# A two-layer hybrid decoder step: conditioning vectors computed one by one, compression units ahead of the first norm, window states copied DRAM to DRAM

## The chip, the cores and the metric

One core of a Trainium2 chip runs the kernel. The metric is the device time of one execution in microseconds; the time before is 1059.74 us, the median of three runs (1058.38 to 1064.3). A profile of one execution gives each engine's instructions with start and duration: PE (TensorE; PEld are its weight loads), DVE (VectorE), ACT (ScalarE), POOL (GpSimd) and SP (the queue that issues most DMAs).

## The reference, cut to what matters

Two layers over 264 token columns: a prompt of 256 and 8 samples of one token. Everything is fp32.

```
mod = silu(c) @ ada_w + ada_b            # (9 rows, 6*1024): sh1, sc1, g1, sh2, sc2, g2
h   = rmsnorm(x) * norm1_g * (1 + sc1) + sh1
proj = h @ w_in                          # q, 6 K/V blocks, gates, z, xBC, dt
kcmp, vcmp = compress(past + new K/V)    # per sample: 32-row blocks, stride 16, two-layer MLP
o_att = gated sum of three branches      # compressed, 16 selected blocks, sliding window of 512
y     = SSD scan over xBC, dt; gated norm with silu(z)
x  += g1 * (concat(o_att, y) @ w_out)
h2  = rmsnorm(x) * norm2_g * (1 + sc2) + sh2
x  += g2 * ((silu(conv3(h2 @ Wg)) * (h2 @ Wu)) @ w_down)
```

Outputs are also the new K/V rows, the scan states, the convolution states, and the sliding-window states of the samples. For the last, the kernel writes the old 512-row window as it is (`wst`, 2 layers x 8 samples of 128x1024, 512 KB each), and the new row is joined to it outside.

## The kernel before, in words

Activations lie as [128 features, 8 blocks, 264 tokens]. A weight tile is 128x1024 (512 KB); it is loaded into one of four `st` buffers, split into a high and a low part (`whi` by ACT, `wlo` by DVE, three buffers each), and used in 24 matmuls of 264 columns (three products for each of eight blocks).

`ada(l, r)` (line 303) computes the conditioning in three rounds r of two vectors each: round 0 gives sh1 and sc1, round 1 g1 and sh2, round 2 sc2 and g2. A round has eight steps, one for each k-block. A step loads four 256 KB tiles and makes four matmuls of 512 columns, each into another quarter of the PSUM partitions (32 columns of the array each, tile `psfl`). Each tile has its own load, buffer and wait. At the end of a round the result is copied (`adam`), transposed by four matmuls and put into `mod`. It is a generator: whoever calls next() on it places one step in the program.

`compress(l, both, bufs)` (line 376) summarizes the compressed-branch pages of the samples in eight units, keys and values in turn for each of four pairs of samples: a unit is 48 matmuls of 252 columns (`pso<-whi,cwh` and two more) and a small second step. With `both` the pages (`cpg`) come with K and V in one load of 128 KB each, 16 loads for a pair, and four buffers. Each of the two weights `cw` is 1 MB.

The order of layer 0: one unit and round 0 of the conditioning, the squares and norm 1; then the input projection (16 tiles `win`; line 462 on), with one unit and one step of round 1 ahead of each tile until they are used up; then the attention stage, where generators for samples (S), prompt (P), scan (M), blocks (B), gating (Z) and conditioning round 2 (A) are interleaved by a written order, `SEQ`; then the output projection, norm 2, and the FFN: up (22 pairs of `wup` tiles; ahead of every second pair one compression unit and one step of round 0 of layer 1), and down (22 `wdn` tiles, five steps of round 1 of layer 1). Layer 1: norm 1, three steps of round 1 (`GAP`), input projection, attention stage with round 2, output projection, norm 2, FFN.

In the attention stage the samples read three sets of eight pages through a ring of eight 512 KB buffers `page`: two sets of selected blocks, 32 loads of 128 KB each set, and the window state, one load for each sample, which is also stored to the output from that buffer (line 606):

```
            if i == 2:
                load(t, I["wst"][l, s])
                store(O["wst"][l, s], t)
```

Loads go through SP, stores through POOL; each engine takes its instructions in one fixed order, made ahead of time by the framework from the program's order and its own estimate of what is ready. Matmuls of other work can therefore stand between the four of one step. In the scan for the samples, four times a layer, DVE writes a masked copy `bd` (8x512, one buffer) that one matmul broadcasts.

Almost all instructions carry line 117, the wrapper that issues them, so the profile is read by tile names.

## Time and profile before

| | |
|---|---|
| time, median of 3 (lowest, highest) | 1059.74 us (1058.38, 1064.3) |
| the profiled execution | 1060.55 us, span 1058.8 us |
| PE busy | 979.6 us (93%) |
| DVE, ACT, POOL busy | 655.8, 486.3, 170.0 us |
| mean granted TensorE clock | 0.949 of full speed |
| DMA | 220.33 MB, mean 208 GB/s |

"Busy" is the time in which an engine has at least one instruction under way. An fp32 matmul leaves two records, the other kind of matmul (high and low parts) one. A row of the chain of waits names what the next instruction in the chain that ended last was held by; "DMA ada" there is the time from issue to landing.

### The profile page before, as it was taken

To read this page: it belongs to the slowest core of one execution; us is meant where nothing else is said; L and a number is where in the kernel's file an instruction comes from. 1 tells how busy PE (TensorE), PEld (TensorE's weight loads), DVE (VectorE), ACT (ScalarE), POOL (GpSimd) and SP (SyncE) were. 2 spreads that over 40 slices of the span, in tenths; PEclk is the share of its full clock that TensorE was granted. 3 is DMA by queue.
4 is the path that set the end of the run, shared out by engine and by line. 5 is a ranking of instruction groups with operands and counts; after the bars stand their busy time and mean duration, and the time that the engine had idled before them with its cause. 6 is when DMAs were issued, how large, how long until landed. Compare 5 with 4: busy or idle time off the path is not lost.

```text
span 1058.8 us, 20737 instructions
## 1 busy us (share of the span) xinstructions
PE 979.6 (93%) x7480; PEld 795.0 (75%) x7480; DVE 655.8 (62%) x1427; ACT 486.3 (46%) x1036; POOL 170.0 (16%) x337
## 2 busy tenths in 40 slices
PE   3799999997997999999999989999799789999996
PEld 3238898652466899899998949965246689999995
DVE  2347554557657865766764558365865777777553
ACT  3225544332254554655553426453235456666441
POOL 0201001114213000101111103031421311111110
PEclk9899999897899899999999999999789889999998
DMA  8779668436847777765577568753694635555651
GB/s 279 262 240 304 227 211 280 162 128 203 333 158 222 225 219 232 255 195 193 185 233 236 165 223 262 250 180 126 207 339 152 208 100 180 181 180 182 195 171 41
DMA packets 115081, 220.33 MB, mean 208 GB/s; under 512 B 13218, under 2 KB 56098, under 8 KB 114850
## 3 DMA queue, kind: packets, MB, share of 16 engines
q1 hardware_dynamic: 110882, 205.29, 60.5%
q0 software_dynamic: 3520, 13.17, 3.1%
q8 instruction: 59, 0.97, 0.4%
q10 hardware_dynamic: 576, 0.54, 0.2%
q14 instruction: 44, 0.36, 0.1%
HBM read 204.70 MB, written 14.25 MB: 207 GB/s over the span
## 4 chain that ended last, share of the span: by engine, by line
PE 82%; DMA 6%; DVE 6%; ACT 2%; issue 2%; SPq 2%; POOL 0%; DVEq 0%; ACTq 0%; POOLq 0%
PE psmm L117 42%; PE psat L117 23%; PE pso L117 10%; PE psfl L117 8%; DMA ada<-in_ada_dram 3%; SPq L117 1%; DMA st<-in_cw_dram 1%; DVE wlo L117 1%; DMA st<-in_wup_dram 1%; DVE bd L117 1%; DMA cpg<-in_cmpc_dram 1%; DVE rs L117 1%; ACT whi L117 1%; DVE psm L117 0%; DVE st L117 0%
## 5 line engine op out<-in xcount | busy, mean ns | idle before, releaser
L117 DVE TENSOR_TENSOR wlo<-st,whi 128x1024 fp32r<-128x1024 f32 (+1 forms) x204 | 232.7, 1141 | 148.8 <-ACT whi L117 132.9
L117 ACT ACTIVATE whi<-st 128x1024 fp32r<-128x1024 f32 (+1 forms) x204 | 201.8, 991 | 231.0 <-PE psmm L117 163.3
L117 PE MATMUL psmm<-hhi,whi 128*128 128x264 f32 x800 | 233.3, 292 | 4.2 <-ACT hhi L117 2.6
L117 PE MATMUL psmm<-hhi,wlo 128*128 128x264 f32 x800 | 228.4, 286 | 0.8 <-DVE wlo L117 0.8
L117 PE MATMUL psmm<-hlo,whi 128*128 128x264 f32 x800 | 228.6, 286 | 0.0
L117 PEld LDWEIGHTS psmm<-hhi,whi 128*128 128x128 f32 x800 | 151.5, 190 | 22.3 <-issue 7.4
L117 PEld LDWEIGHTS psmm<-hhi,wlo 128*128 128x128 f32 x800 | 151.2, 189 | 3.0 <-DVE wlo L117 1.6
L117 PEld LDWEIGHTS psmm<-hlo,whi 128*128 128x128 f32 x800 | 151.9, 190 | 0.9 <-issue 0.7
L117 PE MATMUL psmm<-act,whi 128*128 128x264 f32 x704 | 128.7, 284 | 0.0
L117 PEld LDWEIGHTS psmm<-act,whi 128*128 128x128 f32 x704 | 108.8, 188 | 4.2 <-issue 3.4
L117 PE MATMUL psfl<-ada,cs 128*32 128x512 f32 x384 | 99.3, 648 | 11.0 <-DMA ada<-in_ada_dram 10.9
L117 PE MATMUL psat<-hhi,whi 128*128 128x264 f32 x352 | 100.8, 286 | 1.4 <-ACT whi L117 1.4
L117 PE MATMUL psat<-hhi,wlo 128*128 128x264 f32 x352 | 100.6, 286 | 1.0 <-DVE wlo L117 1.0
L117 PE MATMUL psat<-hlo,whi 128*128 128x264 f32 x352 | 100.5, 286 | 0.0
L117 PE MATMUL psmm<-act,wlo 128*128 128x264 f32 x352 | 99.9, 284 | 0.0
L117 PE MATMUL pso<-whi,cwh 128*128 128x252 f32 x256 | 76.3, 298 | 21.0 <-ACT whi L117 16.2
L117 PE MATMUL pso<-wlo,cwh 128*128 128x252 f32 x256 | 75.5, 295 | 0.1
L117 PE MATMUL pso<-whi,cwl 128*128 128x252 f32 x256 | 75.3, 294 | 0.0
L117 PEld LDWEIGHTS pso<-whi,cwh 128*128 128x128 f32 x256 | 51.3, 200 | 31.6 <-ACT whi L117 16.2
L117 PEld LDWEIGHTS psat<-hhi,whi 128*128 128x128 f32 x352 | 67.1, 191 | 1.6 <-ACT whi L117 1.6
L117 PEld LDWEIGHTS psat<-hhi,wlo 128*128 128x128 f32 x352 | 66.8, 190 | 1.2 <-DVE wlo L117 1.2
L117 PEld LDWEIGHTS psat<-hlo,whi 128*128 128x128 f32 x352 | 67.2, 191 | 0.0
(303 smaller groups left out, 1553.2 us busy)
## 6 DMA issues: line engine op xcount, KB each, us to landing
ada<-in_ada_dram SPq DMA_DIRECT2D x192, 256.0 KB, 4.4
st<-in_wup_dram SPq DMA_DIRECT2D x88, 512.0 KB, 3.6
st<-in_wdn_dram SPq DMA_DIRECT2D x44, 512.0 KB, 3.5
st<-in_win_dram SPq DMA_DIRECT2D x40, 512.0 KB, 4.6
page<-in_slcc_dram SPq DMA_DIRECT2D x128, 128.0 KB, 2.6
st<-in_cw_dram SPq DMA_DIRECT2D x16, 512.0 KB, 5.4
cpg<-in_cmpc_dram SPq DMA_DIRECT2D x64, 128.0 KB, 3.3
st<-in_wout_dram SPq DMA_DIRECT2D x32, 256.0 KB, 3.0
```

The source lines that it names most:

```text
L117: ins = f(*a, **k)
```

## The change

The conditioning is computed by single vectors: `ada(l, js)` takes a list of vectors j of six. A step is now two k-blocks: two tiles of [4, 256] (512 KB each), and eight matmuls of 256 columns, which `together` keeps in order, the last-loaded tile first and the other seven at high priority. The buffers become 3, 2 and 4 of 512 KB where they were 6, 4 and 6 of 256 KB. A vector has four steps, two vectors eight. Vectors 0 and 1 stay ahead of norm 1 of layer 0 and in the FFN-up of layer 0 (for layer 1). Vectors 2 and 3 stay where round 1 was, with four steps in the FFN-down and no `GAP`: the other four come in the input projection of layer 1. Vector 4 is in the attention stage in layer 0 and in the input projection in layer 1; vector 5 is in the FFN-up of its own layer.

Four compression units (keys and values of two pairs of samples) stand ahead of the first norm where one did, with three, three, two and no conditioning steps behind them, and the squares behind the second. The first pair's pages are loaded keys first, values later, 64 KB each. In layer 1 the page ring's pool is opened before the input projection, and one page set is fetched per tile there. The window states are no longer stored from the ring; sixteen DRAM-to-DRAM copies, one for each of the third to eighteenth pairs of the last FFN-up, write them. The scan's four `bd` become two tiles of 8x1024, both written ahead of the loop.

```diff
-ADA_BUFS = {"cmp": 6, "att": 4, "ffn": 6}
+ADA_BUFS = {"cmp": 3, "att": 2, "ffn": 4}
+    def together(calls):
+        for n, (out, w, a, start, stop) in enumerate(calls):
+            if n == 0:
+                PE.matmul(out, w, a, start=start, stop=stop)
+                continue
+            with tc.high_priority():
+                tc.keep_in_program_order(PE.matmul(out, w, a, start=start, stop=stop))
-    def ada(l, r):
+    def ada(l, js):
...
-        acc = fl()
-        for k in range(KC):
-            for g in range(4):
-                t = sb([512], "ada", ADA_BUFS[name[:3]], F32, pools[-2] if name == "attn1" else pools[-1])
-                load(t, I["ada"][l, r * KC + k, :, g, :])
-                PE.matmul(acc[32 * g:32 * g + 32, :], cs[:, k, :], t, start=k == 0, stop=k == KC - 1)
-            yield
+        for j in js:
+            acc = fl()[:, :256]
+            for kk in range(0, KC, 2):
+                two = []
+                for k in (kk, kk + 1):
+                    t = sb([4, 256], "ada", ADA_BUFS[name[:3]], F32, pools[-2] if name == "attn1" else pools[-1])
+                    load(t, I["ada"][l, j, k])
+                    two.append((k, t))
+                together([(acc[32 * g:32 * g + 32, :], cs[:, k, :], t[:, g, :], k == 1, k == KC - 2)
+                          for k, t in reversed(two) for g in range(4)])
+                yield
...
             elif kv == 0:
-                pair = [pages(s, 0) for s in (2 * sp, 2 * sp + 1)]
+                pair = [pages(s, 0, 2 if sp else 1) for s in (2 * sp, 2 * sp + 1)]
+            elif sp == 0:
+                for s in range(2):
+                    load_pages(pair[s][:, :, 1:], I["cmpc"][l], s, 1, 1)
...
+        pb = begin(f"attn{l}") if early is None else None
...
+            if pb is not None and len(ring) < PAGES:
+                fetch()
...
                 load(t, I["wst"][l, s])
-                store(O["wst"][l, s], t)
...
+            bds = [ph([1024], "mam", 2) for _ in range(2)]
+            for g in range(2):
+                V.tensor_tensor(bds[g][:8].rearrange("p (b s n) -> p b s n", b=2, s=NS), ...)
...
-                    bd = small([NS, 64], 1, "bd")
-                    V.tensor_tensor(bd[:8], ...)
-                    PE.matmul(o, ones[:8, :], bd[:8].rearrange("p s n -> p (s n)"), start=True, stop=True)
+                    PE.matmul(o, ones[:8, :], bds[g][:8, 512 * b:512 * b + 512], start=True, stop=True)
...
-        bg = [compress(l + 1, 0, 4), ada(l + 1, 0)] if l + 1 < NL else []
+        bg = [compress(l + 1, 0, 4), chain(ada(l, (5,)), ada(l + 1, (0, 1)))] if l + 1 < NL else [iter(()), ada(l, (5,))]
+        old = [(a, s) for a in range(NL) for s in range(NS)] if l + 1 == NL else []
         for f in range(NFF):
...
+            if old and f >= 2:
+                a, i = old.pop()
+                tc.keep_in_program_order(store(O["wst"][a, i], I["wst"][a, i]))
...
-        rest = ada(l + 1, 1) if l + 1 < NL else iter(())
+        rest = ada(l + 1, (2, 3)) if l + 1 < NL else iter(())
...
-    units, third = compress(0, 1, 4), ada(0, 0)
-    for i in range(FIRST):
+    units, third = compress(0, 1, 4), ada(0, (0, 1))
+    for i in range(len(START)):
         next(units)
...
-    rest = layer(0, A, pa, lambda: units, lambda: end(p0), ada(0, 1), [ada(0, 2)])
+    rest = layer(0, A, pa, lambda: units, lambda: end(p0), ada(0, (2, 3)), [ada(0, (4,))])
     pa = begin("att1")
-    layer(1, pools[-1], pa, None, lambda: None, rest, [ada(1, 2)])
+    layer(1, pools[-1], pa, None, lambda: None, chain(rest, ada(1, (4,))), [])
...
-GAP = (0, 3)
-DOWN = 5
+GAP = (0, 0)
+DOWN = 4
-FIRST, EARLY = 1, 1
+START, EARLY = (3, 3, 2, 0), 1
```

## Rows read from the trace of the kernel before

**Rows 1.** The page's chain that ended last, its shares by engine.

```profile
PE 82%; DMA 6%; DVE 6%; ACT 2%; issue 2%; SPq 2%; POOL 0%; DVEq 0%; ACTq 0%; POOLq 0%
```

**Rows 2.** By stage: length, busy per engine, granted clock, DMA share, GB/s.

```profile
0.00:79.00 79.00, 55.49 (x237) 25.23 (x237) 26.18 (x64) 21.94 (x43) 7.36 (x17) 0.94 0.81 261
79.00:178.00 99.00, 99.00 (x811) 89.20 (x810) 56.40 (x109) 51.12 (x109) 8.54 (x22) 1.00 0.79 253
178.00:309.50 131.50, 119.73 (x898) 65.94 (x897) 79.72 (x216) 49.27 (x154) 32.86 (x57) 0.87 0.61 209
...
610.00:638.00 28.00, 23.69 (x133) 12.37 (x132) 14.68 (x45) 7.52 (x17) 0.36 (x2) 0.94 0.73 242
638.00:683.00 45.00, 45.00 (x375) 45.00 (x374) 30.34 (x54) 25.58 (x48) 10.82 (x21) 1.00 0.86 281
683.00:812.00 129.00, 119.10 (x935) 66.73 (x934) 81.09 (x221) 51.32 (x161) 34.10 (x57) 0.92 0.59 202
...
859.40:981.00 121.60, 121.60 (x1008) 121.60 (x1007) 97.59 (x170) 79.49 (x152) 21.37 (x63) 1.00 0.57 182
```

**Rows 3.** PE on tile psfl (conditioning) in the same stages: length, busy, clock, DMA.

```profile
0.00:79.00 79.00, 29.58 (x84) 0.94 0.81 261
...
178.00:309.50 131.50, 18.91 (x64) 0.87 0.61 209
...
610.00:638.00 28.00, 11.06 (x28) 0.94 0.73 242
...
683.00:812.00 129.00, 16.71 (x64) 0.92 0.59 202
```

**Rows 4.** PE in order of time: one step in one piece, and in pieces.

```profile
47.34 1.05 PE L117 MATMUL psfl<-ada,cs 128*32 128x512 f32 x2
...
91.82 1.07 PE L117 MATMUL psfl<-ada,cs 128*32 128x512 f32 x8
```

**Rows 5.** SP's issues at the start: start, duration, what, count.

```profile
3.96 9.04 SPq L117 DMA_DIRECT2D cpg<-in_cmpc_dram  x16
...
32.95 34.91 SPq L117 DMA_DIRECT2D ada<-in_ada_dram  x32
```

**Rows 6.** DMA issues from 0 to 90 us: count, size, median us to landing.

```profile
ada<-in_ada_dram SPq DMA_DIRECT2D x46, 256.0 KB, 3.7
...
st<-in_cw_dram SPq DMA_DIRECT2D x4, 512.0 KB, 5.6
```

**Rows 7.** The chain of waits, from the start to the first units: start, duration.

```profile
17.71 7.83 DMA ada<-in_ada_dram
...
75.99 4.56 PE psmm L117 x29
...
92.88 5.79 PE pso L117 x48
```

**Rows 8.** Three single stretches of 20 us, columns as in Rows 2.

```profile
80.00:100.00 20.00, 20.00 (x170) 18.30 (x169) 14.92 (x41) 11.50 (x28) 2.25 (x6) 1.00 0.95 309
...
660.00:680.00 20.00, 20.00 (x168) 20.00 (x167) 9.30 (x9) 9.16 (x14) 1.48 (x4) 1.00 0.97 328
```

**Rows 9.** The chain of waits where the attention stage of layer 0 begins.

```profile
179.82 6.31 DMA ada<-in_ada_dram
```

**Rows 10.** Waits of PE in the attention stages, layer 0: total, times, longest.

```profile
PE psfl L117 <- DMA ada<-in_ada_dram: 4.4, 2, 2.4
PE psat L117 <- DVE bd L117: 3.3, 2, 2.2
```

**Rows 11.** POOL around the window states of layer 0, in order of time.

```profile
276.13 0.53 POOL L606 DMA_DIRECT2D out_wst_dram<-page  x1 [9.99 <-DMA page<-in_wst_dram]
...
290.93 1.56 POOL L117 TENSOR_SCALAR psc<-psc,psm 128x256 f32<-128x256 f32 x3
```

**Rows 12.** PE around norm 1 of layer 1: the roots' broadcast, the steady projection.

```profile
621.44 1.64 PE L117 MATMUL psmm<-cst,rs 128*128 128x128 f32 x6
...
637.88 0.37 PE L117 MATMUL psmm<-hhi,whi 128*128 128x264 f32 x1
```

More of the change, by code (lines that the diff above doesn't have):

```diff
@@ L301, in run @@
             pass
-    def ada(l, r):
-        if r == 0:
+    def ada(l, js):
+        if l not in MOD:
             MOD[l] = sb([48, 9], "mod", 2)
@@ L390, in weights, with pages @@
             W[kv] = (whi, wlo)
-        def pages(s, kv):
+        def pages(s, kv, n):
             t = ph([NPG, 2 if both else 1, 128], "cpg", bufs)
-            load_pages(t, I["cmpc"][l], s, 0 if both else kv, 2 if both else 1)
+            load_pages(t[:, :, :n], I["cmpc"][l], s, kv, n)
             return t
@@ L474, in layer, with slot, fetch @@
             next(side, None)
+        pb = begin(f"attn{l}") if early is None else None
+        def slot(tag, shape, dt=F32):
+            return sb(shape, tag, dict(whi=WB[0], wlo=WB[1], st=WB[2])[tag], dt)
+        order = (0, 2, 4, 6, 1, 3, 5, 7)
+        ring = []
+        def fetch():
+            n = len(ring)
+            i, s = n // NS, order[n % NS]
+            if i > 2:
+                return
+            t = ph([1024], "page", PAGES)
+            if i == 2:
+                load(t, I["wst"][l, s])
+                v = t.rearrange("p (a c f) -> p a c f", a=2, c=4)
+                ring.append((v[:, 0], v[:, 1]))
+            else:
+                v = t.rearrange("p (c a f) -> p c a f", a=2, c=4)
+                load_pages(v, I["slcc"][l], s, 0, 2, 4 * i, 4)
+                ring.append((v[:, :, 0, :], v[:, :, 1, :]))
         first = iter(()) if early is None else early()
@@ L585, in layer @@
         run(side)
-        done()
-        pb = begin(f"attn{l}")
-        def slot(tag, shape, dt=F32):
-            return sb(shape, tag, dict(whi=WB[0], wlo=WB[1], st=WB[2])[tag], dt)
-        order = (0, 2, 4, 6, 1, 3, 5, 7)
-        ring = []
-        def fetch():
-            n = len(ring)
-            i, s = n // NS, order[n % NS]
-            if i > 2:
-                return
-            t = ph([1024], "page", PAGES)
-            if i == 2:
-                load(t, I["wst"][l, s])
-                store(O["wst"][l, s], t)
-                v = t.rearrange("p (a c f) -> p a c f", a=2, c=4)
-                ring.append((v[:, 0], v[:, 1]))
-            else:
-                v = t.rearrange("p (c a f) -> p c a f", a=2, c=4)
-                load_pages(v, I["slcc"][l], s, 0, 2, 4 * i, 4)
-                ring.append((v[:, :, 0, :], v[:, :, 1, :]))
+        if pb is None:
+            done()
+            pb = begin(f"attn{l}")
         def samples():
@@ L638, in samples @@
             V.tensor_copy(slf, selfp[:, :2])
-            for _ in range(PAGES):
+            while len(ring) < PAGES:
                 fetch()
@@ L1183, in layer @@
         AL = [ph([KC, T], "act", 6, F32R) for _ in range(3)]
-        bg = [compress(l + 1, 0, 4), ada(l + 1, 0)] if l + 1 < NL else []
+        bg = [compress(l + 1, 0, 4), chain(ada(l, (5,)), ada(l + 1, (0, 1)))] if l + 1 < NL else [iter(()), ada(l, (5,))]
+        old = [(a, s) for a in range(NL) for s in range(NS)] if l + 1 == NL else []
         for f in range(NFF):
             if f % 2 == 0:
-                for b in bg:
-                    for _ in range(1 + UNITS * (f == 0 and b is bg[0])):
-                        next(b, None)
+                next(bg[0], None)
+            if f % 2 == 0 or f < 4:
+                next(bg[1], None)
             o = mtile(I["wup"][l, 2 * f], h)
@@ L1301, in _layout @@
     A["cT"] = ca(c.reshape(32, KC, 128).transpose(2, 1, 0))
-    A["ada"] = ca(f["ada_w"].reshape(NL, KC, 128, 3, 2048).transpose(0, 3, 1, 2, 4)).reshape(NL, 24, 128, 4, 512)
+    A["ada"] = ca(f["ada_w"].reshape(NL, KC, 128, 6, 4, 256).transpose(0, 3, 1, 2, 4, 5))
     A["adab"] = ca(f["ada_b"].reshape(NL, 48, 128).transpose(0, 2, 1))
```

38 lines of the change are left out of this document (18 added, 20 removed).

## The prediction

> **What bounds it now.** I read the chain of waits first: PE holds 82% of it [rows 1]. So what counts is PE's time and the places where PE stands. The table by stage shows where: the input projections (79 to 178 and 638 to 683 us) and the last FFN-up run PE without a gap at full clock, while the start (55.5 of 79 us busy), the two attention stages (119.7 of 131.5 and 119.1 of 129.0) and norm 1 of layer 1 (23.7 of 28) leave PE idle, and the attention stages also run at a clock of 0.87 and 0.92 [rows 2]. Then I read the same stages for the conditioning's tile alone: 29.6 us of the start, 18.9 and 16.7 of the attention stages, 11.1 of norm 1 [rows 3]. PE in order of time says why it is so much: a step whose eight records come in one piece takes 1.07 us, but two records alone, one matmul of the four, take 1.05 us [rows 4]. Four matmuls side by side in the array cost what one costs; before, they are only side by side when all four tiles happen to have landed.
>
> **Price of a step.** A step has the same columns before and after (4 x 512, or 8 x 256 in four strips). I take 1.07 us for a step, that is 4.3 us for a vector, plus 0.3 us for its two transposes: 4.6 us. From below nothing makes it shorter than 1.07; from above, a step that does not stay together costs up to 4 x 1.05 = 4.2 us.
>
> **The start (0 to 79 us).** PE loses 29.6 - 9.2 = 20.4 us of conditioning and gets three units of 5.8 us [rows 7], 17.4 us plus their small second steps. So PE has no more to do; the loads decide. By volume: 16.9 MB must land ahead of the norm (conditioning 8.4, pages 4.2, `cw` 2.1, the rest 2.2); at the stage's 261 GB/s [rows 2] that is 65 us, at the 309 GB/s of the next 20 us [rows 8] 55 us. From the last conditioning matmul to steady matmuls at 76 us [rows 7] some 8.5 us pass now, so 63 to 73 us. By buffers: with three buffers a pair's last load is issued only when the pair before it is used up. The first tile lands at 25.5 us (17.7 + 7.8) [rows 7]; then eight pairs of issue 0.4, landing 3.7 to 5.6 [rows 6] and 1.07 us make 41 to 57 us, and steady matmuls at 75 to 91. Between 63 and 91 I take 75, the short end of the second, because SP's 32 conditioning issues spread over 34.9 us [rows 5] wait for matmuls that go away: a gain of 1 us, bounds 13 gained, 15 lost. The split first pages cost 16 more SP issues at 9.04/16 = 0.57 us [rows 5], 9 us; they fit into that waiting.
>
> The Trainium skill ("DMA: Bandwidth & Descriptors", Rules for kernel authors) tells to coalesce, since transfers under 64 KB pay mostly overhead; the halved pages are just 64 KB. By that rule the 32 halves would cost as much as 32 whole pages, 2.1 MB at 261 GB/s, 8 us more at the start. No row here shows a 64 KB page; the sum stands without this.
>
> **Input projection, layer 0.** PE is full for 99 us [rows 2]; three units fewer are 17.4 us and some 2 us of second steps. By the end of this stage 0.261 x 79 + 0.253 x 99 = 45.7 MB have come [rows 2]; to bring them 18 us sooner takes 285 GB/s from the start on, under the 309. I take 16 us; bounds 19 and 3 (at 261 GB/s the bytes need 175 us of 178).
>
> **Attention stages.** Layer 0 has 18.9 us of conditioning and 4.4 us of PE waiting for its tiles [rows 3, 10], and keeps one vector, 4.6: 18.7 us go. Layer 1 loses all 16.7. PE is busy in nine tenths of these stages, so most of it is really on its path, but chains through DVE (80 of 130 us busy) come out behind it: I take three quarters, 14 and 12.5; bounds one third and all.
>
> **Window states.** The store waits in POOL's queue for the load: POOL stands 10 us for the first of eight, and the prompt's `psc` scaling behind them ends after 291 us [rows 11]. Load and store, 4.2 MB each way, also share the DMA. Without the store both come free; between 0 and 8 us a layer I take 2.5, so 5 us. The copies return in the last FFN-up: 16 x 0.5 MB read and written over 16 pairs of 5.5 us (121.6/22 [rows 2]) add up to 190 GB/s to 182. That is past 328 [rows 8] if reads and writes count alike, and the weights have four buffers, about two pairs, in front. Their issue on POOL, 0.53 us each [rows 11], waits for nothing and POOL is busy 21 of 122 us. I take 2 us lost, bounds 0 and 10.
>
> **`bd`.** PE waits 3.3 us for it in layer 0 [rows 10], as the one buffer is written between other DVE work. Both tiles early leave one wait, for a tile twice as wide. I take 3 us for both layers, bounds 0 and 6.
>
> **Norm 1, layer 1.** From the roots' broadcast at 621.4 to the projection's steady matmuls at 637.9 [rows 12] PE does little but conditioning, 11 us in this stage [rows 3]. It goes; DVE and ACT still have to write the normalized tiles. I take 7 us, bounds 3 and 11.
>
> **What comes in elsewhere.** The input projection of layer 1 gets eight steps, 8.6 + 0.6 = 9.2 us on a full PE. Its loads: 0.242 x 28 + 0.281 x 45 = 19.4 MB from 610 to 683 [rows 2], less three old steps and plus eight, 24.7 MB in about 75 us, 329 GB/s, just the 328 of its best 20 us [rows 8]. And with two buffers a step's pair is loaded only after the step before; matmuls behind it on PE wait with it. I take 6 us, bounds 0 and 23 (24.7 MB at 253 GB/s need 98 us). FFN-up of layer 0: one vector more, 4.6, and FFN-down one step less, 1.1: 3.5 us lost. Last FFN-up: 4.6 us lost.
>
> **The sum.** Gained 1 + 16 + 14 + 12.5 + 5 + 3 + 7 = 58.5; lost 2 + 9.2 + 6 + 3.5 + 4.6 = 25.3; net 33.2 us. The profiled execution took 1060.55 us, 0.8 over the median shown; 1060.55 - 33.2 = 1027.3, which is 1026.5 on the median's scale. I say 1027.
>
> **Rivals.**
> *Transfers take back the units* (0.14). The start runs by buffers (5 us lost instead of 1 gained) and the projection behind it by bytes (3 gained for 16): 19 us less, 1046 us. For it: DMA shares of 0.81 and 0.79 over 178 us [rows 2]. Against: PE never stood in that projection.
> *The clock falls in attention* (0.07). The attention stages are where the clock falls, to 0.87 and 0.92, while stages with PE full have 1.00 [rows 2]; less matmul work may lower it further. At 0.75 in both, the share of half speed, twice what is missing, rises from 26 and 16% to 50%, and half of that time is lost: 0.12 x 115 + 0.17 x 114 = 33 us if PE set the pace, about 25 with what DVE covers: 1052 us. The Trainium skill ("TensorE: Matmul & The Clock Gate", HAM oscillation) says that waits between bursts of matmuls put the array at half rate. By it, the same 1052; rows 2 agree in that every stage under 1.00 has idle PE. Against: the conditioning steps themselves bring waits for DMA there.
> *Slower: the pairs stop PE* (0.07). Twelve steps have just two buffers (four in attention 0, eight in the projection of layer 1). PE takes its matmuls in order; if each stands for its landing, as the step at 179.8 did for 6.3 us [rows 9], twelve times 6.3 is 76 us for the 6 allowed: 1097 us. It decides against the change from (33 + 6)/12 = 3.3 us a step. Against: in the projection of layer 0 eight such steps cost PE no idle time [rows 2].
> *All of the attention work comes free* (0.10): the last quarter, the window states' other 11 us and some of the start, 30 us together: 997 us.
> *The steps don't stay together*, so that the change does not do what it says: the 48 steps would then cost up to 4.2 us each, 150 us more than taken; that eight records in a row took 1.07 us [rows 4] speaks against it (0.01, slower).
>
> **How the numbers follow.** The forecast, with its own range of 1008 to 1043 (each large term off by a third of its bounds, one against another), has 0.57; all of attention coming free 0.10, transfers 0.14, the clock 0.07. Half of each of these two together ends at 1050 to 1065, no change: 0.04. The pairs 0.07 and the scattered steps 0.01 are slower. A measurement of this kernel tells 0.5%, 5 us, from no change, hardly less. So faster 0.57 + 0.10 + 0.14 + 0.07 = 0.88, same 0.04, slower 0.08. The range 1000 to 1052 holds the forecast, the transfers, half of the clock's case and a part of the fullest: it leaves out about 2 in 10.
>
> **What would show it.** Conditioning records in pieces of eight, some 53 us in all for 103; four units before the first steady matmul, and that at 70 to 80 us; the projection of layer 0 some 80 us long; no conditioning in attention 1, and both attention stages 12 to 18 us shorter at a clock not below 0.85; no wait of POOL for `page`; the projection of layer 1 at 55 to 62 us with waits for `ada` under 8 us. Wrong would make it: steady matmuls after 85 us, PE waits for `ada` over 3 us a step, or a clock near 0.75 in attention.

## The result: slower, 1115 us for 1059

The changed kernel takes 1115.34 us (median of 4, 1112.59 to 1117.22), the kernel before 1059.06 beside it: a ratio of 1.052, 95% interval 1.048 to 1.056. The forecast was 1027 with a range of 1000 to 1052. The profiled execution took 1115.4 us, its span is 1113.6. Here and below a ratio is formed without the executions that were disturbed, a median with all of them.

The page's chain that ended last, its shares by engine; before, PE held 82% of it [rows 1]:

```profile
PE 70%; DMA 11%; DVE 9%; ACT 5%; issue 2%; SPq 2%; POOL 0%; DVEq 0%; ACTq 0%; POOLq 0%
```

The table by stage of the changed kernel (start, projection 0, attention 0, FFN-up 0, projection 1, attention 1, last FFN-up; columns as in [rows 2]). An attention stage runs here from its first scores to the roots of norm 2 (the inverse roots `rs` that PE broadcasts), with the output projection in it; the projection of layer 1 runs from the roots of norm 1, and so holds that norm:

```profile
0.00:108.50 108.50, 59.36 (x423) 42.59 (x424) 34.99 (x81) 30.57 (x62) 7.32 (x17) 0.78 0.74 242
108.50:197.30 88.80, 87.30 (x787) 78.68 (x782) 49.49 (x97) 43.53 (x92) 7.87 (x22) 1.00 0.66 218
197.30:357.20 159.90, 140.57 (x1086) 93.28 (x1076) 106.57 (x296) 65.00 (x184) 38.97 (x58) 0.88 0.49 168
357.20:559.70 202.50, 199.40 (x1703) 187.95 (x1703) 138.55 (x251) 116.05 (x230) 21.53 (x65) 0.97 0.69 228
633.70:709.70 76.00, 71.45 (x617) 60.24 (x618) 41.62 (x89) 33.81 (x70) 9.93 (x21) 0.95 0.79 273
709.70:861.00 151.30, 133.81 (x1059) 88.32 (x1048) 101.05 (x292) 62.74 (x180) 37.11 (x58) 0.88 0.46 157
861.00:1035.20 174.20, 149.59 (x1096) 141.09 (x1097) 101.74 (x182) 82.57 (x156) 26.77 (x77) 0.93 0.54 181
```

Between the same instructions in both traces (a stage's first or last matmul), the length before, after, and the difference. A gate tile is one of the small matmuls of 32 columns from `st` that come right behind a norm:

| stage, to its end | before | after | us |
|---|---|---|---|
| start, to the last gate tile of norm 1 | 78.8 | 108.5 | +29.7 |
| projection, layer 0 | 100.8 | 88.9 | -11.9 |
| attention and output projection, layer 0 | 168.3 | 159.8 | -8.4 |
| FFN-up, layer 0 | 196.9 | 202.6 | +5.7 |
| FFN-down, layer 0, to the roots of norm 1 | 76.8 | 74.0 | -2.8 |
| norm 1 and projection, layer 1 | 67.9 | 76.0 | +8.1 |
| attention and output projection, layer 1 | 158.9 | 151.3 | -7.6 |
| last FFN-up | 132.6 | 174.3 | +41.7 |
| end | 77.9 | 78.4 | +0.4 |

Two stages lose 71 us; the seven others together gain 16. In the last FFN-up PE is busy 149.6 of 174.2 us, where it was full [rows 2], and the granted clock is 0.93 over the stage, 0.97 before. The conditioning did get cheaper, 63.0 us of PE in all for 103.0 (tile psfl, PE busy in the start, attention 0, projection 1, attention 1; 29.6, 18.9 and 16.7 us in the start and the two attentions before [rows 3]):

```profile
0.00:108.50 108.50, 14.36 (x148) 5.06 (x148) 0.47 (x2) 0.75 (x2) 0.78 0.74 242
197.30:357.20 159.90, 3.59 (x50) 1.50 (x50) 0.22 (x1) 0.37 (x1) 0.88 0.49 168
...
633.70:709.70 76.00, 10.97 (x132) 4.14 (x132) 0.47 (x2) 0.77 (x2) 0.95 0.79 273
709.70:861.00 151.30, 2.53 (x32) 1.05 (x32) 0.00 (x0) 0.00 (x0) 0.88 0.46 157
```

The 32 records in attention 1 are two steps of the vector that the program places in the last FFN-up: they ran ahead of it, at 850.9 and 854.1 us.

**The last FFN-up** first. ACT in order of time there in the kernel before, one pair:

```profile
925.86 1.06 ACT L117 ACTIVATE whi<-st 128x1024 fp32r<-128x1024 f32 x1 [1.51 <-PE psmm L117]
926.83 0.41 ACT L117 ACTIVATE act<-s 128x264 fp32r<-128x264 f32 x1
927.14 0.44 ACT L117 ACTIVATE xr<-psmm 128x256 f32<-128x256 f32 x2
927.61 0.62 ACT L117 ACTIVATE xa<-xr,halfw 128x280 f32<-128x280 f32 x1
928.76 1.06 ACT L117 ACTIVATE whi<-st 128x1024 fp32r<-128x1024 f32 x1 [0.53 <-PE psat L117]
929.73 0.42 ACT L117 ACTIVATE s<-xa 128x280 f32<-128x280 f32 x1
```

and one period of the changed kernel:

```profile
925.89 1.06 ACT L117 ACTIVATE whi<-st 128x1024 fp32r<-128x1024 f32 x1 [4.18 <-PE psat L117]
926.85 0.50 ACT L117 ACTIVATE xr<-psmm 128x256 f32<-128x256 f32 x3
927.32 1.14 ACT L117 ACTIVATE xa<-xr,halfw 128x280 f32<-128x280 f32 x2
...
932.70 0.36 ACT L117 ACTIVATE xr<-psmm 128x256 f32<-128x256 f32 x1
933.32 1.06 ACT L117 ACTIVATE whi<-st 128x1024 fp32r<-128x1024 f32 x1 [0.26 <-PE psmm L117]
936.63 1.06 ACT L117 ACTIVATE whi<-st 128x1024 fp32r<-128x1024 f32 x1 [2.25 <-PE psat L117]
941.86 1.06 ACT L117 ACTIVATE whi<-st 128x1024 fp32r<-128x1024 f32 x1 [4.16 <-PE psat L117]
```

A period is 16 us and holds two pairs (two `xa`, two of every tile), where a pair took 5.8 before, two 11.6 (the 1008 matmuls in 121.6 us [rows 2] are 21 pairs of 48). PE runs two `psmm` tiles and then two `psat` tiles, ACT splits three weights in a row and waits 4.2 us for the tile that frees the next buffer. POOL puts two pairs together too:

```profile
927.34 0.92 POOL L117 COPY fout<-xr 128x26 f32<-128x26 f32 x1 [17.59 <-ACT xr L117]
928.21 0.49 POOL L1221 DMA_DIRECT2D out_wst_dram<-in_wst_dram  x1
928.69 0.22 POOL L117 COPY fout<-xr 128x26 f32<-128x26 f32 x1
928.83 0.49 POOL L1221 DMA_DIRECT2D out_wst_dram<-in_wst_dram  x1
```

The copy's issue itself waits for nothing and takes 0.49 us; a copy lands in 5.4 us (median). No engine's wait in this stage ends with a DMA. So the theory was: the order that the framework wrote for all engines changed with the copies. The rival: the copies' 8.4 MB read and 8.4 MB written beside the weights.

**The start.** PE's conditioning pairs and the norm behind them, in order of time:

```profile
39.39 1.93 PE L117 MATMUL psfl<-ada,cs 128*32 128x256 f32 x16 [2.82 <-DMA ada<-in_ada_dram]
...
63.41 1.93 PE L117 MATMUL psfl<-ada,cs 128*32 128x256 f32 x16 [4.42 <-DMA ada<-in_ada_dram]
...
84.47 1.93 PE L117 MATMUL psfl<-ada,cs 128*32 128x256 f32 x16 [8.09 <-DMA ada<-in_ada_dram]
...
93.20 0.82 PE L117 MATMUL psat<-cst,row 1*128 1x1 f32 x6
...
98.35 1.13 PE L117 MATMUL psmm<-cst,rs 128*128 128x128 f32 x6 [1.99 <-DVE rs L117]
...
108.46 0.82 PE L117 MATMUL psmm<-hlo,st 128*32 128x264 f32 x5
```

The last pair comes at 84.5 and ends at 86.4, and from there 22.1 us pass to the last gate tile. In the kernel before, the last conditioning matmul ended at 67.5, and 11.3 us passed to the same tile. So of the 29.7 us lost 18.9 are a later conditioning and 10.8 a longer tail. Besides the wait for its first weights, which is the same 16.2 us in both, PE waits 16.0 us in the start for conditioning (1.6 before) and 14.2 for `hid`, a tile of the units' small second steps (4.8 before). SP's issues say what was loaded between the pairs:

```profile
42.95 8.70 SPq L117 DMA_DIRECT2D cpg<-in_cmpc_dram  x16
...
53.88 3.49 SPq L117 DMA_DIRECT2D cpg<-in_cmpc_dram  x7
57.77 0.81 SPq L117 DMA_DIRECT2D ada<-in_ada_dram  x2
...
69.91 3.25 SPq L117 DMA_DIRECT2D cpg<-in_cmpc_dram  x5
73.21 1.13 SPq L117 DMA_DIRECT2D st<-in_win_dram  x2
75.44 3.79 SPq L117 DMA_DIRECT2D cpg<-in_cmpc_dram  x7
80.41 0.81 SPq L117 DMA_DIRECT2D ada<-in_ada_dram  x2
```

The rows at 53.9 and 69.9 are pages of the third pair of samples, that at 75.4 of the fourth: they go ahead of the conditioning that the norm waits for. Theory: their place in SP's order, and PE's order behind the last pair. Rival: three buffers, as the prediction's second estimate had it.

### The profile page after: what moved, and what is told of

Its sections match the earlier page's. It is cut to its first block, busy times and chain, and to the rows that moved or that the text cites. A ratio compares the mean times of both kernels' runs of the same rounds, so it can differ in the third digit from the quotient of the medians.

```text
span 1113.6 us, 21377 instructions
## 1 busy us (share of the span) xinstructions
PE 980.0 (88%) x7864; PEld 825.3 (74%) x7864; DVE 651.4 (58%) x1429; ACT 488.2 (44%) x1042; POOL 168.0 (15%) x337
## 4 chain that ended last, share of the span: by engine, by line
PE 70%; DMA 11%; DVE 9%; ACT 5%; issue 2%; SPq 2%; POOL 0%; DVEq 0%; ACTq 0%; POOLq 0%
PE psmm L117 35%; PE psat L117 22%; PE pso L117 8%; DMA ada<-in_ada_dram 5%; PE psfl L117 4%; DVE wlo L117 4%; ACT whi L117 3%; DMA st<-in_cw_dram 3%; SPq L117 1%; DMA st<-in_wup_dram 1%; DVE xa L117 1%; DMA st<-in_win_dram 1%; DVE rs L117 1%; DVE s L117 1%; DMA page<-in_wst_dram 1%
## 5 line engine op out<-in xcount | busy, mean ns | idle before, releaser
L117 PEld LDWEIGHTS psmm<-hhi,whi 128*128 128x128 f32 x800 | 152.5, 191 | 29.8 <-ACT xr L117 11.1
L117 PE MATMUL psat<-hhi,whi 128*128 128x264 f32 x352 | 105.0, 298 | 10.6 <-ACT whi L117 10.6
L117 PE MATMUL psat<-hhi,wlo 128*128 128x264 f32 x352 | 105.5, 300 | 7.5 <-DVE wlo L117 7.1
L117 PE MATMUL psat<-hlo,whi 128*128 128x264 f32 x352 | 103.8, 295 | 0.0
L117 PE MATMUL pso<-whi,cwh 128*128 128x252 f32 x256 | 77.6, 303 | 22.5 <-ACT whi L117 16.2
L117 PEld LDWEIGHTS psat<-hhi,whi 128*128 128x128 f32 x352 | 70.4, 200 | 12.5 <-ACT whi L117 12.5
L117 PEld LDWEIGHTS psat<-hhi,wlo 128*128 128x128 f32 x352 | 70.2, 199 | 10.9 <-DVE wlo L117 10.8
L117 PE MATMUL psfl<-ada,cs 128*32 128x256 f32 x768 | 57.8, 421 | 21.0 <-DMA ada<-in_ada_dram 21.0
L117 POOL COPY fout<-xr 128x26 f32<-128x26 f32 x44 | 27.4, 624 | 301.6 <-ACT xr L117 301.6
```

The costliest lines, as they stand in the source:

```text
L117: ins = f(*a, **k)
```

## The experiments

All runs are on the changed kernel unless said otherwise; times are medians beside runs of the kernel before (1056.1 to 1058.4). Times in each expectation are on the same scale.

**The copies on another queue, or tiny.**

```diff
-                tc.keep_in_program_order(store(O["wst"][a, i], I["wst"][a, i]))
+                tc.keep_in_program_order(nc.sync.dma_start(O["wst"][a, i], I["wst"][a, i]))       # c_sp
+                tc.keep_in_program_order(store(O["wst"][a, i][:1], I["wst"][a, i][:1]))           # c_tiny
```

> The changed kernel, with the sixteen copies of the window states issued by SP instead of POOL, at the same places of the program and still kept in order. The same bytes move at the same time; what changes is the order made for PE and POOL, in which the two tiles of a pair of the last FFN-up alternate again. If the order is the cause (PE two tiles of one kind, then two of the other, with two buffers each, so that it stands while ACT works), the last FFN-up takes about 137 us (132.6 before plus 4.6 for one vector) for 174, and the kernel 1078 us. If the transfers of the copies are the cause, 170 to 175 us there and 1111 to 1117 us. If SP is held by the copies so that weights come late, something between, with PE waiting for st.

> The changed kernel with the sixteen copies at their places on POOL but of one row of 4 KB each instead of 512 KB; the rest of the window states is left out. There is next to no traffic, POOL issues as many copies as before, and the order of PE alternates again. By the order and by the transfers alike 137 us for the last FFN-up and 1078 us in all. If POOL's issuing itself were the cause (sixteen issues in its queue between the small copies), it would stay at 170 to 175 us and 1111 to 1117 us.

On SP: 1193.42 us (ratio 1.129, 1.123 to 1.134), the stage 250.4 us. Neither theory had that. PE alternated, but ACT and DVE had yet another order: PE waits for `whi` 16 times, 58 us, and no engine's wait ends with a DMA there either. So this run doesn't tell the two theories apart. Tiny (which leaves the rest of the window states unwritten): 1073.93 us (1.016, 1.012 to 1.021), the stage 133.8 us, which both theories allow. The stage with the tiny copies, and ACT in it, again one pair in 5.8 us and in the order of the kernel before:

```profile
859.70:993.50 133.80, 133.79 (x1096) 131.56 (x1097) 104.61 (x190) 84.21 (x161) 28.57 (x79) 0.98 0.56 172
```

```profile
932.72 1.06 ACT L117 ACTIVATE whi<-st 128x1024 fp32r<-128x1024 f32 x1 [1.51 <-PE psmm L117]
933.69 0.41 ACT L117 ACTIVATE act<-s 128x264 fp32r<-128x264 f32 x1
...
935.62 1.06 ACT L117 ACTIVATE whi<-st 128x1024 fp32r<-128x1024 f32 x1 [0.53 <-PE psat L117]
936.59 0.42 ACT L117 ACTIVATE s<-xa 128x280 f32<-128x280 f32 x1
```

The two splits of a pair stand apart, with the pair's activations between them. POOL issues as many copies as in the changed kernel, so its issuing is not the cause.

**Full copies, order given for some engines, then for all four.**

```diff
+        if old:
+            pinned.update(("PE", "POOL"))                       # c_pe; at the loop's end pinned.clear()
```
```diff
+        ws = [wsplit(wtile(I["wup"][l, n])) for n in range(2)]  # c_pipe, c_pipet (tiny copies)
+        pinned.update(("PE", "DVE", "ACT", "POOL"))
         for f in range(NFF):
-            o = mtile(I["wup"][l, 2 * f], h)
+            o = mm()
+            gemm8(o[:, :T], ws.pop(0), h)
...
+            ws.append(wsplit(wtile(I["wup"][l, 2 * f + 2])))    # ahead of Tanh
...
+            ws.append(wsplit(wtile(I["wup"][l, 2 * f + 3])))    # ahead of the last split
```

> The changed kernel with the copies full and on POOL as they are, and PE's and POOL's instructions of the last FFN-up kept in the order of the program: tiles of the two kinds alternate on PE, each pair's small copies alternate on POOL. Order theory: the last FFN-up about 137 us, the kernel 1078 us, like the copies on SP. Transfers: 170 to 175 us there, 1111 to 1117 us. If the copies hold POOL's queue: the same 170 or more, with POOL waiting at its issues.

> The changed kernel with the last FFN-up written out in a pipelined order (the split of a later weight tile stands between the activations of a pair, as in the kernel before) and PE, DVE, ACT and POOL kept in that order; the sixteen copies are full, on POOL, at the places they have. With PE and POOL alone kept in order the stage still took 158 us, but then ACT and DVE stood in another order than with the 4 KB copies, and no engine waited for a DMA. If the orders of the engines are the whole cause, this kernel takes 137 to 140 us for the last FFN-up and 1073 to 1080 us in all, like the one with the 4 KB copies (1073.9). If the transfers cost the time, 155 us or more there and 1095 us or more.

> The same written-out order with copies of 4 KB (the rest of the window states is left out). Every engine has the same order as in the run with the full copies, so the difference of the two is the transfers alone: 0 to 3 us by the order theory, 20 us or more by the transfers. Its own last FFN-up: 137 to 140 us, the kernel 1072 to 1079 us.

With PE and POOL in order: 1107.87 us (1.048, 1.043 to 1.053), the stage 162.4 (the 158 in the expectation of c_pipe is not what this trace shows). Only 12 of 40 us came back; ACT now did `xr xa s act whi whi`, both splits behind the pair. That looked like the traffic, but with all four engines in order full and tiny copies give the same (c_pipet, too, leaves the rest of the window states unwritten): 1090.25 (1.033, 1.027 to 1.038) and 1093.79 us (1.030, 1.026 to 1.035). Attention 0 and the last FFN-up, full copies:

```profile
203.70:358.10 154.40, 133.08 (x1082) 88.05 (x1072) 106.72 (x296) 65.21 (x184) 39.06 (x58) 0.93 0.52 175
858.10:1009.30 151.20, 142.18 (x1128) 133.98 (x1129) 104.11 (x191) 87.70 (x162) 22.16 (x81) 0.98 0.70 217
```

and with copies of 4 KB:

```profile
200.60:365.00 164.40, 147.32 (x1084) 93.62 (x1073) 106.34 (x296) 65.09 (x184) 38.93 (x58) 0.83 0.48 162
864.40:1015.50 151.10, 141.46 (x1129) 133.03 (x1130) 104.13 (x192) 87.45 (x162) 22.10 (x81) 0.99 0.53 161
```

151.2 and 151.1 us, at 217 and 161 GB/s, with the same instructions in the same order on PE, DVE, ACT and POOL: under this order the transfers cost nothing. So the 40 us are the order, as far as a stage can show it in which PE still stands 9 us; beside a full PE the traffic was not tried in this stage. My written order is itself 17 us worse than the framework's with tiny copies (the forecast of 137 to 140 was missed; two more conditioning steps stand in it).

**The start: fewer units ahead, whole pages.**

```diff
-START, EARLY = (3, 3, 2, 0), 1
+START, EARLY = (8,), 1                     # s_one; squares behind run(third)
```
```diff
-                pair = [pages(s, 0, 2 if sp else 1) for s in (2 * sp, 2 * sp + 1)]
+                pair = [pages(s, 0, 2) for s in (2 * sp, 2 * sp + 1)]    # s_whole; with s_one: s_one_whole
```

> The changed kernel with one compression unit ahead of the first norm instead of four, all eight conditioning steps behind it, and the squares behind these; everything else as changed, three buffers too. Counted in SP's order, 16.1 MB stand ahead of and with the sixteenth conditioning tile, 21.3 MB in the changed kernel, where pages of the second to fourth pair come between. If these bytes set the first norm (21.3 MB at 261 GB/s are 82 us, and the last pair stood at 85), the last pair of layer 0 comes at about 62 us and the norm's gate tiles end at 75 to 80 for 108; the projection behind it takes its three units back, 100 us for 89. The kernel: 1115 less 30 and plus 12, 1097 us. If three buffers for pairs set it (each pair loaded only when one before it is used), the last pair stays at 80 to 85 us, the gate tiles at 95 or later, and the kernel gets no shorter, 1112 to 1125 us.

> One unit ahead of the first norm as before, and the first pair's pages whole (16 loads of 128 KB) instead of keys first and values later (32 of 64 KB). If SP's sixteen issues more, some 0.57 to 0.6 us each, hold up the conditioning's loads, the first norm comes up to 9 us earlier than with the halves (gate tiles at 72 to 80 us for 79.6) and the kernel takes 1098 to 1106 us. If the bytes in SP's order set it, it comes later: 18.8 MB stand up to the sixteenth tile instead of 16.1, 10 us at 261 GB/s, gate tiles at 85 to 90 us and the kernel 1107 to 1115 us.

> The changed kernel with its four units ahead of the norm, and only the first pair's pages whole. With one unit ahead the whole pages made the stages to attention 0 11 us shorter (178.5 for 189.5), though more bytes stood ahead of the conditioning. If SP's sixteen issues more are the reason, the same holds with four units: gate tiles at 98 to 103 us for 108.5, and the kernel 1105 to 1109 us. If it was the order that PE got with one unit, nothing changes here: gate tiles at 106 to 111, 1112 to 1118 us.

One unit: 1106.89 us (1.047, 1.042 to 1.051), the last pair at 65.5 and the gate tiles at 79.6, as the bytes in SP's order said and the buffers didn't. But the projection behind took 109.9 us, not 100. With whole pages too: 1088.42 us (1.031, 1.026 to 1.035); the gate tiles are as early (79.5) and the projection takes 99.0. By the expectation 2.7 MB more stood ahead of the last pair, and it came 2.1 us later (67.6), not 10. Whole pages with four units hardly change the gate tiles: 107.8, 1107.49 us (1.046, 1.040 to 1.052). So neither of my two readings of the pages holds: SP's issues are not what held the norm, and the bytes ahead of a pair don't set it alone. What differs is the projection's first 20 us, PE and its clock with halves, one unit:

```profile
79.60:100.00 20.40, 20.40 (x141) 17.85 (x140) 12.85 (x37) 9.77 (x24) 1.17 (x3) 0.78 0.61 200
```

and with whole pages:

```profile
79.50:100.00 20.50, 20.50 (x182) 17.89 (x182) 14.32 (x42) 11.19 (x28) 1.81 (x6) 1.00 0.77 259
```

41 instructions fewer in the same time at a clock of 0.78; 33 matmuls more of the units had also been done ahead of it with whole pages. With halves PE had waited 18.2 us for conditioning by then, with whole pages 8.9. Why was not taken apart. Of the 18.5 us between the two medians, some 7 are attention 0 by the profiles (163.7 at a clock of 0.85, 156.5 at 0.92), which the edit doesn't touch.

**Two causes in the start, one at a time.**

```diff
         if i == 1:
             for k in range(KC):
                 square(k)
+            ROOTS.extend(inv_roots(SUMS[-1], 1, 1.0 / D))      # a_roots; norm 1 takes them from there
```
```diff
-START, EARLY = (3, 3, 2, 0), 1
+START, EARLY = (8, 0, 0, 0), 1            # front_roots; squares, roots behind the first unit's steps,
+                                          # whole pages, ring stores, layer 1 as in best_ring
```

> The changed kernel with one thing moved: the roots of the first norm are made right behind the squares, ahead of the third and fourth unit, and not behind the fourth. In the changed kernel's trace 22 us pass from the last conditioning pair to the last gate tile: what is left of the fourth unit (6.1 us), the transposes of its result and of the conditioning (1.5), the roots (93.3 to 99.5), then the gate tiles. If the order of PE behind the last pair is what makes this tail, the gate tiles end 5 to 7 us earlier, at 101 to 104 us for 108.5, and the kernel takes 1106 to 1111 us. If the roots were hidden (the normalized tiles wait for the conditioning's own transposes and additions anyway), nothing changes, 1113 to 1118 us.

> Four units ahead of the norm as changed, but all eight conditioning steps behind the first of them, with the squares and the roots behind these, so that in SP's order the pages of the second pair and of those after it follow the conditioning: the sixteenth tile stands at 17 to 18 MB instead of 21.3. First pages whole, window states from the ring, layer 1 as in best_ring (1053.2, start 81.2 and attention 0 at 180.3). If the place of the conditioning's loads in SP's order set the last pair, it comes at 66 to 72 us instead of 85; with the three units behind it on PE (some 12 us left of them) the gate tiles end at 86 to 92 us and attention 0 starts 85 to 89 us later, at 173 to 180 us. If four units delay the pairs in whatever order (PE or the DMA engines take the time), the last pair stays at 80 us or more, the gate tiles at 100 or more and attention 0 at 188 to 198 us.

Early roots: gate tiles at 102.3 for 108.5, 1101.43 us (1.044, 1.040 to 1.047): PE's order makes some 6 us of the tail. Conditioning ahead of the later units: 1052.37 us (0.995, 0.991 to 0.999), the last pair at 68.5 for 84.5,

```profile
68.50 1.07 PE L117 MATMUL psfl<-ada,cs 128*32 128x256 f32 x16 [1.18 <-DMA ada<-in_ada_dram]
```

and the gate tiles at 91.7, both as SP's order said. The edit moves the conditioning ahead of the units in PE's program as well, so that it doesn't tell SP's queue from PE's. And attention 0 begins at 184.7, outside 173 to 180: the projection took 93 us for 85 to 89. With one unit and whole pages it begins at 178.5 to 180.4, with two at 180.3, before at 179.5. Four units ahead paid in none of these runs.

**Layer 1's conditioning back, and the copies elsewhere.**

```diff
-GAP = (0, 0)
+GAP = (0, 3)                                                  # g_att
-    layer(1, pools[-1], pa, None, lambda: None, chain(rest, ada(1, (4,))), [])
+    layer(1, pools[-1], pa, None, lambda: None, rest, [ada(1, (4,))])
```
```diff
+        for a, i in old:                                      # best, best_two: behind the last FFN-up
+            tc.keep_in_program_order(store(O["wst"][a, i], I["wst"][a, i]))
+                store(O["wst"][l, s], t)                      # best_ring: from the ring, as before
```

All of best, best_two and best_ring have g_att's edit and whole pages; one unit ahead, but best_two has two, `START = (4, 4)`.

> The changed kernel with two things of layer 1 put back where they were: three conditioning steps ahead of the input projection instead of in it, and the vector 4 of layer 1 in the attention stage. The input projection of layer 1 loses 7 of 8 steps' worth of crowding: from the roots of norm 1 to attention 1 76.0 us come back toward the 67.9 of before, and attention 1 toward its 158.9 from 151.3. If moving conditioning out of attention only moves its time (what the projection loses the attention stage gains), the kernel stays within 5 us of the changed one, 1110 to 1120 us. If conditioning in a stage short of loads costs more than in attention, it gets 5 to 10 us shorter, 1105 to 1110; if attention was the dearer place, 5 to 8 longer, 1120 to 1123 us.

> Three parts of the changed kernel put back, the rest kept: one unit ahead of the first norm and whole first pages; three conditioning steps ahead of the input projection of layer 1 and its vector 4 in the attention stage; the sixteen copies full, on POOL, but all issued behind the loop of the last FFN-up, so that its order is that of the kernel before. If the losses are where the stages showed them, they come off one by one: 1088.4 (one unit, whole pages) less 40.4 for the last FFN-up (174.2 to 133.8 as with the 4 KB copies) less 7 to 9 for the input projection of layer 1 (g_att: 66.6 for 76.0) makes 1040 us, between 1034 and 1047, below the kernel before. If the copies' 8.4 MB, now beside the weights of the last FFN-down, hold that stage (64 us with 11.5 MB of weights), it gets 10 to 30 us longer and the kernel 1050 to 1070 us.

> As the one before, with two units ahead of the first norm (keys and values of the first pair of samples), four conditioning steps behind each. If each unit ahead of the norm delays it as much as it later takes off the projection (SP's bytes and PE's time both only move), the start gets 5 to 8 us longer, the projection of layer 0 6 us shorter, and the kernel stays within 3 us of the one with one unit. If units there use time in which PE waits for conditioning anyway, 4 to 6 us shorter.

> As the first of these, with the window states stored from the ring of pages in the attention stages, as in the kernel before, instead of the sixteen copies. If POOL's waits for the page and the store's traffic cost the attention stages something (5 us in all was forecast, 0 to 16), the attention stages are 2 to 4 us longer each than with the copies behind the FFN-up, and the kernel is 3 to 8 us longer less what the copies cost in FFN-down. If the store was hidden there, the two are equal within 3 us.

g_att: 1119.06 us (1.060, 1.054 to 1.065), but stage by stage it says more: projection 1 took 66.6 us for 76.0, and attention 1 with its vector

```profile
713.80:863.90 150.10, 132.38 (x1112) 87.22 (x1100) 104.31 (x293) 63.76 (x181) 37.99 (x58) 0.94 0.54 183
```

150.1 for 151.3 without it, at a clock of 0.94 for 0.88. What took that gain away is most of all attention 0, 167.5 us at 0.82 for 159.8 at 0.88, which the edit doesn't touch: its instructions stand in the same order on PE, DVE, ACT and POOL in both traces. So its total can't be read as the price of the edit, and my three cases for it weren't told apart by it.

best: 1066.18 us (1.004, 1.000 to 1.008). The last FFN-up is back at 133.5, yet the copies now stand beside the last FFN-down's weights,

```profile
973.60:1050.40 76.80, 69.19 (x530) 67.95 (x528) 30.83 (x47) 24.13 (x29) 15.77 (x24) 0.93 0.69 231
```

where it takes, with the copies in the ring,

```profile
971.70:1035.60 63.90, 63.90 (x530) 63.90 (x528) 30.95 (x47) 24.15 (x29) 8.81 (x8) 1.00 0.49 145
```

13 us less, with the same order of PE, DVE and ACT: sixteen copies at once are not free. ACT waits 20.3 us there for weights (`st<-in_wdn_dram`), and not at all with the ring. best_two: 1066.38 (1.012, 1.006 to 1.018), its start and projection each within 0.2 us of best's. So the second unit made the start no longer and the projection no shorter, where the expectation had them move by 5 to 8 and by 6 us. best_ring: 1053.24 us (1038.72 to 1060.79; no interval).

**What is left of the change.**

```diff
+    rest = layer(0, A, pa, lambda: units, lambda: end(p0), ada(0, (2, 3)), [ada(0, (4, 5))])   # v_att, final
+    layer(1, pools[-1], pa, None, lambda: None, rest, [ada(1, (4, 5))])                        # v_att
+    layer(1, pools[-1], pa, None, lambda: None, rest, [ada(1, (4,))])                          # final
+        bg = [compress(l + 1, 0, 4), ada(l + 1, (0, 1))] if l + 1 < NL else [iter(()), ada(l, (5,))]  # final
```

(on best_ring; in v_att the last FFN-up has no conditioning), and b_bd: the kernel before with only the two tiles of masked copies (`bds`) written ahead of the loop.

> As best_ring, with the fourth and fifth conditioning vector of both layers in the attention stage, where the kernel before has them, so that what is left of the change is the step by vectors (eight matmuls kept together) and the two early masked copies. Forecast theory: a vector costs PE 4.6 us, of which three quarters count in attention; the attention stages get 3 to 4 us longer than with one vector (150 to 157 us, by the clock of the execution), FFN-up of layer 0 5 us shorter (202.6 to 197), the last FFN-up up to 1 shorter: 1 to 4 us faster than best_ring's 1053.2. If a vector in the attention stage costs nothing, because PE waits there anyway and the steps keep its clock up, 6 to 8 us faster, 1045 to 1047. If the steps stop PE there (two buffers), attention 10 us or more longer in each layer, 1065 or more.

> The kernel before with one part of the change: the two masked copies of the scan for the samples, written ahead of the loop. Forecast theory: 3 us in both layers together, between 0 and 6, so 1053 to 1055 us where the kernel before takes 1056 to 1059; PE's 3.3 us of waiting for the copy in attention 0 are gone. If the wait only hid another one, no change.

> As v_att (1049.5), with the last vector of layer 1 back in the last FFN-up, so that attention 1 has one vector and attention 0 two. In the last FFN-up that vector cost 0.3 us (133.8 with it, 133.5 without). If attention with one vector runs 3 to 5 us shorter than with two at the same clock, 1045 to 1047 us. If one vector or two makes no difference there (the clock and the gaps take it), 1048 to 1051 us.

v_att: 1049.53 us (0.994, 0.992 to 0.997), FFN-up of layer 0 198.2 for 202.6. The total is what its first case said, but attention 0 took 163.9 us, outside that case's 150 to 157. b_bd: 1056.26 us (0.999, 0.996 to 1.002). PE's waits for the copy fell from 3.3 us [rows 10] and 2.5 to 1.8 (below) and 0.4 in the two attention stages,

```profile
PE psat L117 <- DVE mam L117: 1.8, 1, 1.8
```

and 3 us are less than this interval can tell. final: 1045.91 us (0.988, 0.984 to 0.992), 1.2% below the kernel before and the fastest here. It has the new step, one unit ahead, whole pages, the ring's stores, the early masked copies, and one vector of layer 1 in the last FFN-up. That it came out at 1045 to 1047 speaks for a dearer second vector in attention 1; the medians of v_att and final overlap in their single times, so this is not shown.

## Why the prediction was wrong, point by point

**Last FFN-up: the step that failed most.** That the copies' issue on POOL "waits for nothing" was right for the issue (0.49 us), and the transfers were hidden too. The step gave the copies 2 us and took the rows of the old order for granted: the kernel's engines run in an order that is made anew for the changed program, and this is where 40 us went (174.2 us, 133.8 with tiny copies, 151 for full and tiny alike under one order). PE stands 24.6 us of this stage and none of it with tiny copies; the other 15.8 us it is busy longer with the same work, at a clock of 0.93 for 0.98. Between the changed kernel and the tiny copies only the copies' size differs, which leaves the framework's estimate of them as what wrote the other order; the estimate itself no run shows. The vector cost this stage 0.3 us (133.8 with, 133.5 without) for 4.6, but two of its four steps ran ahead of it, in attention 1, so that 0.3 is not the price of a vector. The prediction's 5.5 us a pair were 5.8: its window holds 21 pairs, not 22.

**The start.** A gain of 1 us, bounds 13 and -15, was a loss of 29.7. Both estimates failed. By volume I counted 16.9 MB ahead of the norm; in SP's order 21.3 MB stood up to the sixteenth tile, with pages of the third and fourth pair and two `win` tiles in it. By buffers, eight pairs in 41 to 57 us from 25.5 on, the last pair was to end at 67 to 82 us; it ended at 86.4. The step that failed there counts pairs that follow one another with nothing between: with three buffers kept, but the conditioning ahead of the later units, the last pair ended at 67.4 (one unit) and 69.6 (four), inside that estimate. The other 10.8 us are the tail. It was copied from the kernel before, but behind the last pair PE now had the rest of a unit and the roots (6 us of it came back with early roots). How much of the later conditioning is SP's order and how much PE's own is not settled.

**Projection, layer 0.** 16 forecast, 11.9 measured. So the start and this stage together lost 17.8 us; with one unit and whole pages they came to 178.5, 1 us from before. The units ahead bought nothing.

**Price of a step.** Right: 16 records in 1.07 us, 1.93 where the granted clock was 0.50, the lower of its two levels. Nine steps in the start took 14.4 us, where 84 records took 29.6. The prediction took 9.2 us off for two vectors there, at full clock; but PE stood more ahead of the norm, and the clock was 0.78 for 0.94 [rows 2], which the prediction weighed for attention alone.

**Attention.** For the two stages 18 and 16.5 us were forecast, 14 and 12.5 of them for the conditioning, the rest for window states and `bd`; 8.4 and 7.6 came, at a clock of 0.88 for 0.87 and 0.88 for 0.91. One profile tells such a gain only roughly: the same orders of the changed attention 0 took 156.5 us at 0.91 in c_tiny and 167.5 at 0.82 in g_att, and b_bd, the kernel before but for the masked copies, took 158.7 at 0.95 where that took 168.3 at 0.87. In layer 1 without vector 4 the stage took 147.0 to 152.5 us at 0.87 to 0.91 in ten executions (mean 149.3); with it 148.6 to 150.1 at 0.94 and 0.95 in three, and 152.5 at 0.91 and 157.0 at 0.88 (mean 151.5): 2.2 us for a vector of 4.6. At a like clock it is some 5 us: 152.5 (best) for 147.5 (s_whole) at 0.91, 157.0 (front_roots, which stores from the ring) for 151.3 (the changed kernel) at 0.88. By these few rows the clock's rival had its mechanism half right: without the vector PE saves there about its 4.6 us, and the clock, lower without it, takes about half of that back. The Trainium skill ("TensorE: Matmul & The Clock Gate", HAM oscillation) says that PE's waits between bursts of matmuls throttle it; these rows agree in direction, as the clock is lower where PE has less to do. The rival's 0.75 in both stages did not come.

**Window states.** 5 us forecast. best (copies later) and best_ring have attention 0 at 161.4 and 164.4 us, both at 0.85; best_two and front_roots (ring) at 156.3 and 156.7. Between runs at a like clock the store from the ring costs 0 to 3 us in this stage; not settled.

**`bd`.** 3 forecast, 0.1% measured with an interval of 0.4% below to 0.2% above no change: unresolved, and small.

**Norm 1 and projection, layer 1.** 7 gained and 15.2 lost were forecast, net 8.2 lost; 8.1 was measured, but that is luck, as both terms were too large. From the roots' broadcast to the steady matmuls, 621.4 to 637.9 before [rows 12], it is 633.7 to 646.5 in the changed kernel: 12.8 for 16.4 us, 3.7 gained, with two of the new steps still in it. With three steps put back ahead of the projection (g_att) it is 11.6, so moving them out gave nothing. The projection behind then lost 11.8 for 15.2, with PE waiting 3.6 us for conditioning.

**FFN of layer 0.** 3.5 lost forecast, 2.9 measured: 5.7 lost in FFN-up, of which its vector is 4.4 (198.2 us without it, 202.6 with), and 2.8 gained in FFN-down.

Set right, the two failed terms turn -33.2 into -33.2 + 30.7 (start, 29.7 lost for 1 gained) + 35.1 (last FFN-up, 41.7 for 6.6) = +32.6; the other terms were to give 38.8 net and gave 16.5, which makes the 54.9 between the two traces.

**The rivals.** The slower one, pairs that stop PE, did not decide: of its twelve steps those in attention 0 cost PE no wait, those in the projection of layer 1 3.6 us, not the 39 it needs. Transfers taking back the units was the nearest, but not by their rate: it was 242 GB/s over the start, under the 261 before [rows 2].

## What to carry to other kernels

An edit that "waits for nothing" still enters the plan that orders every engine: compare the order of the new program's engines with the old one's around it before the old durations are carried over. Work put ahead of a point on the path can stand in the queues of what that point waits for: read those queues in order, the loads' and PE's, up to that point, and don't count only what the point needs. And work taken out of a stage with waits isn't gained in full: a vector was worth 2.2 us in attention 1 on average, and 4.4 in the full FFN-up of layer 0.

## What the runs showed of the hardware

The same orders of PE, ACT, DVE and POOL took 154.4 us at a clock of 0.93 and 164.4 at 0.83 in attention 0, in two executions whose kernels differ only in the size of copies 500 us later. Twelve executions of best lay between 1053.5 us at a mean clock of 0.946 and 1075.5 at 0.919. A difference of 10 us in such a stage, in one profile, says nothing without its clock. A DRAM-to-DRAM copy of 512 KB took 0.49 us to issue on POOL and 5.4 us to land; sixteen of them cost nothing spread over a stage of 151 us in which PE stood 9, and 13 us when issued together beside a stage that loads 145 GB/s of weights.
